# Second-product expert weights in row pairs, and the usual order for the last two experts

## The chip, the cores and the metric

The kernel runs on one core of a Trainium2 chip. The metric is the device time of one launch in microseconds (us); lower is better. The core has five engines with a queue of instructions each: TensorE (PE, its weight loads are PEld), VectorE (DVE), ScalarE (ACT), GpSimd (POOL) and SyncE (SP). SP does no arithmetic here and issues nearly all transfers from memory; 16 DMA engines carry them out.

## What is computed

One layer of a diffusion backbone on 256 tokens (128 of a prompt, 128 of a sample) of width 1024: a mixer (state-space scan and convolution), then a mixture of 32 experts of which each token uses 4, then a final norm. The change touches the experts alone:

```python
def expert_step(acc, e):
    w_gu_e, b_gu_e, w_down_e, b_down_e, w_tok = e
    g, u = jnp.split(t @ w_gu_e + b_gu_e, 2, axis=-1)      # first product, 1024 x 2048
    g = jnp.minimum(g, SWIGLU_LIMIT)
    u = jnp.clip(u, -SWIGLU_LIMIT, SWIGLU_LIMIT)
    act = (u + 1.0) * g * jax.nn.sigmoid(SWIGLU_ALPHA * g)
    out = act @ w_down_e + b_down_e                        # second product, 1024 x 1024
    return acc + w_tok[:, None].astype(out.dtype) * out, None
```

All weights are float32: 12 MB for each expert, 384 MB in all.

## The kernel before

The mixer takes the first 485 us or so, the experts the rest. Of each expert only the tokens routed to it are computed: `gather_slots` picks up to 64 of them for a pair of experts by a matmul with a 0/1 matrix (`xg`). Then, for expert e, `expert_up` makes the first product (line 1238, tiles `e..pgu`, 64 matrix products of 128x64 by 128x512 as the trace counts them, and four for the bias at line 1243), `overflow` tests on every engine whether more tokens are left (a branch, line 1343; the pass behind it runs for expert 11 alone in this trace), and `expert_act` makes `gm` on DVE and ACT (lines 1251 to 1255). `gm` holds 64 tokens by 1024 channels as 128 partitions by 512: the upper 64 partitions are the second half of the channels.

`transposed` (lines 1286 and 1287) turns `gm` round with four PE transposes into the PSUM tile `e..pat`, and ACT copies that to `e..aT`. `down_products` (line 1299) makes the second product into `e..py`, 32 matrix products as the trace counts them. `keep_y` (line 1307) copies `py` into the tile `y` of the pair, one half on ACT and one on DVE. `scatter_pair` (line 1274, tile `pst`, copied to `sT`) and `add_pair` (line 1314, tiles `e..pc`, added into `xT` by DVE at line 1184) put a pair's results back to their tokens. In the usual order the second product of expert e-1 stands on PE ahead of the first product of expert e, and the results of a pair are put back two experts later. From expert 2 on a scheduler sets the order on the engines at build time; `finale` is written out by hand for PE.

The weights come in pieces of 1 MB, twelve to an expert, into 22 slots that are used in turn: pieces 0 to 7 are 128 rows of the first matrix (8 KB on each partition in one run), pieces 8 to 11 are 256 rows of the second. A second-product piece has rows p and p+128 of its 256 on partition p, so two runs of 4 KB. SP issues piece after piece; each issue waits until the piece eight issues back has landed and until the slot is free.

The last two experts are different. The order of the loads is: first product of 30, first product of 31, second product of 30, second product of 31. The second matrix of expert 31 comes by columns: each of its four pieces holds two blocks of 128 columns and all 1024 rows, in 512-byte runs, by four transfers. `finale` makes the first product of 31 ahead of the second product of 30, and then the second product of 31 in four column blocks (`down_rows`, line 1479, tile `lastpy`). After each block `finish` copies it to `y`, puts 256 columns back to their tokens (line 1488, tile `pcl`), adds them into `xT` on DVE, and squares (line 1491, tile `sql`) and scales `xT` (lines 1495 on ACT, 1497 on POOL). So `finish` of one block runs beside the products of the next. Then come the sums of the squares (`pssl`), the norm's factor on POOL (`rf`, line 183), its broadcast (`rbf`), the last multiplications on DVE and five stores.

Of the kernel before, what the change touches and what calls it, by code (L numbers as in the profile page):

```python
# [63 lines left out]
def hybrid_step(ctx, tc, A):  # L64
# [314 lines left out]
    def load_piece(e, c, t=None):  # L379
        if t is None:  # L380
            t = ready.pop((e, c), None)
            if t is not None:
                npc[0] += 1
                return t
            t = next_slot(f"w{e}_{c}")
        if c < 8:
            npc_ins[0] = nc.sync.dma_start(t, w_gu[0, e, c * P:(c + 1) * P, :])
            return t.unsqueeze(1)
        if e == NE - 1:

            t = t.rearrange("p (i k n) -> p i k n", i=2, n=P)
            for k in (0, 4):
                for i in range(2):
                    c0 = (c - 8 + 4 * i) * P
                    nc.sync.dma_start(t[:, i, k:k + 4], w_dn[0, e, k * P:(k + 4) * P, c0:c0 + P].rearrange("(k p) n -> p k n", p=P))
            return t
        t = t.rearrange("p (k n) -> p k n", k=2)
        src = w_dn[0, e, (c - 8) * 256:(c - 7) * 256, :].rearrange("(k p) n -> p k n", p=P)
        nc.sync.dma_start(t, src)
        return t  # L400

    def open_slots(n):
# [12 lines left out]
    early = [0, 1, 2, NSLOT - 3, NSLOT - 2, *range(3, NSLOT - 3)]  # L415

    def load_expert(e):

        if e == NE - 1:
            return last_up + [load_piece(e, c) for c in range(8, 12)]  # L420
        w = [load_piece(e, c) for c in range(8)]
        if e == NE - 2:
            last_up.extend(load_piece(e + 1, c) for c in range(8))
        return w + [load_piece(e, c) for c in range(8, 12)]

    last_up = []
    first_in = []

    def weight_blocks():
# [742 lines left out]
    sm = ctx.enter_context(tc.tile_pool(name="sm", bufs=1))  # L1172

    open_slots(NSLOT - 3 - len(mx))
    def down_cols(e, w, k, c0, wd):

        if e == NE - 1:
            return [w[8 + c // P % 4][:, c // 512, k, :] for c in range(c0, c0 + wd, P)]
        return [w[8 + k // 2][:, k % 2, c0:c0 + wd]]

    def add_gated(k, s, x):

        sl = slice(s * P, (s + 1) * P)
# [96 lines left out]
    def transposed(gm, name, m, tag="aT", bufs=1):  # L1280

        wd = D * m // P
        pat = bank("E", name + "pat", 1)[:, 0:wd]
        aT = sm.tile([P, 512], F32, name=name + "aT", tag=tag, bufs=bufs)[:, 0:wd]
        for c in range(wd // P):
            PE.transpose(pat[:, c * P:(c + 1) * P], gm[:, c * P:(c + 1) * P], ident)  # L1286
        S.copy(aT, pat)  # L1287
        return [aT[:, a:a + m] for a in (k * P % wd + k * P // wd * m for k in range(KC))]

    def down_products(e, at, w, py, m, swap, ks=range(KC)):  # L1290

        nq = P // m
        wd = D // nq
        for k in ks:
            for q in range(nq):
                parts = down_cols(e, w, k, (q ^ swap) * wd, wd)
                n = wd // len(parts)
                for i, part in enumerate(parts):
                    last = PE.matmul(py[m * q:m * q + m, i * n:(i + 1) * n], at[k], part,  # L1299
                                     start=(k == 0 and i == 0), stop=(k == KC - 1), skip_group_check=True)  # L1300
        return last

    def keep_y(ys, py, swap, cols=slice(0, 512)):
# [45 lines left out]
    def overflow_pass(e, w, over, n):  # L1349
        m, nq, wd = OVER, P // OVER, D * OVER // P  # L1350
        V.tensor_scalar(over, over, -float(OVER), None, op0=ALU.add)

        gx = sm.tile([P, 2, m], F32, name=f"gx{n}", tag="g1", bufs=1)
        for s in range(2):
            V.tensor_scalar(gx[:, s], iof[:, 0:m], over[:, s:s + 1], None, op0=ALU.is_equal)
        px = bank("C", f"px{n}", 2)
        for s in range(2):
            for q in range(nq):
                PE.matmul(px[m * q:m * q + m, 0:wd], gx[:, s], h2[:, s, q * wd:(q + 1) * wd],
                          start=(s == 0), stop=(s == 1), skip_group_check=True)  # L1360
        xs = sm.tile([P, wd], F32, name=f"xs{n}", tag="um", bufs=1)
        V.tensor_copy(xs, px[:, 0:wd])
        pxt = bank("C", f"pxt{n}", 2)
        for c in range(wd // P):
            PE.transpose(pxt[:, c * P:(c + 1) * P], xs[:, c * P:(c + 1) * P], ident)
        xo = sm.tile([P, nq, wd // P, m], F32, name=f"xo{n}", tag="xg", bufs=2)
        S.copy(xo, pxt[:, 0:wd].rearrange("p (c q s) -> p q c s", q=nq, s=m))
        go = expert_act(expert_up(e, xo.rearrange("p q c s -> p (q c) s"), w, over_banks(f"{n}pgu", 2), m), n, m, tag="go")
        sg = sm.tile([P, 2, nq, m], F32, name=f"so{n}", tag="um", bufs=1)
        slots_of([sg[:, s] for s in range(2)], e, [over[:, s:s + 1] for s in range(2)])  # L1370
        pst = bank("E", f"pso{n}", 1)
        for s in range(2):
# [5 lines left out]
        down_products(e, transposed(go, n, m), w, py, m, 0)  # L1378
# [15 lines left out]
    def new_y(e):  # L1394
        return [sm.tile([P, 512], F32, name=f"y{e}{q}", tag=f"y{q}", bufs=1) for q in range(2)]

    def down(e):
        if e % 2 == 0:
            ys[e] = new_y(e)
        gm, w = acts.pop(e)  # L1400
        py = bank("D", f"e{e}py", 1)
        last = down_products(e, transposed(gm, f"e{e}", CAP), w, py, CAP, e % 2)
        keep_y(ys[e - e % 2], py, e % 2)
        return last

    def up(e):
# [6 lines left out]
    def expert(e):  # L1413
# [28 lines left out]
        if e % 2 == 0:  # L1442
            if e:
                last = add_pair(e - 2)
            if e == 24:
                add_bias()
        else:
            gather_slots(e + 1)

    w = last = mores = None  # L1450
    for e in range(NE - 1):

        with tc.manual_schedule(engines={mybir.EngineType.PE}) if e < 2 else ExitStack():
            expert(e)


    def finale():
        e = NE - 1
        w = load_expert(e)
        gm, w_1 = acts.pop(e - 1)  # L1460
        banks = expert_up(e, xgs.pop(e), w, up_banks(e, f"e{e}pgu"), CAP, last)
        overflow(e, w, mores[e % REGS])
        at_1 = transposed(gm, f"e{e - 1}", CAP, "xg", 2)
        gm = expert_act(banks, f"e{e}", CAP)
        y = new_y(e - 1)
        py = bank("D", f"e{e - 1}py", 1)
        down_products(e - 1, at_1, w_1, py, CAP, 0, range(4))
        at = transposed(gm, f"e{e}", CAP, "xg", 2)
        down_products(e - 1, at_1, w_1, py, CAP, 0, range(4, KC))
        keep_y(y, py, 0)  # L1470
        pss = bank("E", "pssl", 1)
        py = [bank("BD"[c % 2], f"lastpy{c // 2}", 1) for c in range(2)]
        products = pair_products(scatter_pair(e - 1), y)
        sq = next_slot("sql").rearrange("p (k t) -> p k t", t=T)

        def down_rows(c, ks):
            for k in ks:
                for q in range(2):
                    PE.matmul(py[c % 2][CAP * q:CAP * (q + 1), c * P:(c + 1) * P], at[k], w[8 + c][:, 1 - q, k, :],  # L1479
                              start=(k == 0), stop=(k == KC - 1), skip_group_check=True)  # L1480

        def finish(c):

            cs = slice(c * P, (c + 1) * P)
            keep_y(y, py[c % 2], 1, cs)
            pc = bank("C", f"pcl{c}", 2)
            for i, k in enumerate((c, c + 4)):
                PE.matmul(pc[:, i * T:(i + 1) * T], *products[k], start=True, stop=True)  # L1488
# [23 lines left out]
        down_rows(3, range(KC))  # L1512
        finish(2)
        finish(3)
        for k in (0, 2, 6, 3, 7):
# [97 lines left out]
```

## Time and profile before

| what | us |
|---|---|
| median of 3 runs (lowest, highest) | 1470.7 (1467.85, 1472.33) |
| the profiled execution, its own time | 1469.36 |
| its span, first to last instruction | 1467.6 |
| PE busy in the span | 1352.0 (92%) |
| DVE, ACT, POOL busy | 593.2, 338.1, 108.3 |
| read from memory | 498.26 MB, 343 GB/s over the span |

A busy PE in this table is not PE at its peak, since the ends of pipelined matrix products are modelled. A wait is listed with the engine that waited and what ended it; a name with a q is an engine's queue of instructions, which branches, issues and waits while the engine itself is idle. PEclk is the granted clock of TensorE as a share of 2.4 GHz: 1.00, or 0.50 at its lower level of 1.2 GHz.

### The profile page before, as it was taken

How to read it: one execution, taken by the hardware profiler on the slowest of the kernel's cores; microseconds unless marked ns; L12 is line 12 of the kernel's file. 1: busy time of each engine (PE TensorE's matmuls, PEld its weight loads, DVE VectorE, ACT ScalarE, POOL GpSimd, SP SyncE). 2: the span in 40 equal slices, each digit the busy share in tenths (PEclk: the TensorE clock that was granted, in tenths of full speed). 3: DMA queues.
4: the chain of work that ended last, by engine and by line, in shares of the span. 5: the costliest groups of instructions: out<-in, count | busy, mean ns of one | idle time of the engine just before them, and what ended most of it. 6: DMA issues, size and time to landing. Idle time of an engine off the chain costs nothing. (4 is left out here: it accounts for less than half of the span.)

```text
span 1467.6 us, 21473 instructions
## 1 busy us (share of the span) xinstructions
PE 1352.0 (92%) x8627; PEld 799.2 (54%) x8627; DVE 593.2 (40%) x1265; ACT 338.1 (23%) x636; POOL 108.3 (7%) x121
## 2 busy tenths in 40 slices
PE   6998999999999899999999779999899999989997
PEld 3887989889999443443343334343433343334434
DVE  4864879897776312222132113212312123221323
ACT  2544656565754110000010000000000000000102
POOL 1112314421002100000000000000000000000001
PEclk9999999999999899999999988999999999999998
DMA  9996565646897799999999699999999999999993
GB/s 367 281 275 190 194 239 212 244 167 210 316 327 290 289 407 411 415 412 416 416 413 415 269 372 382 416 416 416 413 414 417 415 415 415 416 415 417 415 365 111
DMA packets 132359, 506.48 MB, mean 345 GB/s; under 512 B 9827, under 2 KB 45283, under 8 KB 94307
## 3 DMA queue, kind: packets, MB, share of 16 engines
q1 hardware_dynamic: 129314, 497.72, 87.4%
q10 hardware_dynamic: 2880, 6.60, 1.3%
q8 instruction: 99, 1.62, 0.5%
q14 instruction: 66, 0.53, 0.1%
HBM read 498.26 MB, written 5.64 MB: 343 GB/s over the span
## 5 line engine op out<-in xcount | busy, mean ns | idle before, releaser
L291 DVE TENSOR_TENSOR wl<-win,wh 128x1024 fp32r<-128x1024 f32 (+1 forms) x84 | 101.2, 1216 | 33.7 <-ACT wh L290 28.3
L290 ACT CAST wh<-win 128x1024 fp32r<-128x1024 f32 (+1 forms) x84 | 83.9, 1009 | 73.0 <-PE pbc L318 19.2
L1501 POOL TENSOR_TENSOR sql<-sql 128x256 f32<-128x256 f32 x3 | 2.2, 727 | 971.1 <-ACT sql L1491 971.1
L711 POOL TENSOR_TENSOR m<-m_half,adt 128x512 fp32r<-128x512 f32 x32 | 43.2, 1368 | 86.6 <-PE pss L714 86.6
L318 PE MATMUL pxs<-hT,wh 128*128 128x256 f32 x256 | 37.5, 291 | 0.0
L318 PE MATMUL pz<-hT,wh 128*128 128x256 f32 x256 | 37.3, 291 | 0.0
L318 PE MATMUL pgt<-hT,wh 128*128 128x256 f32 x256 | 36.0, 287 | 0.6 <-ACT wh L290 0.6
L318 PE MATMUL pbc<-hT,wh 128*128 128x256 f32 x256 | 35.6, 287 | 0.0
L318 PEld LDWEIGHTS pxs<-hT,wh 128*128 128x128 f32 x256 | 32.5, 190 | 3.6 <-issue 2.8
L318 PE MATMUL pso<-yhl,wh 128*128 128x256 f32 x256 | 34.1, 284 | 0.0
L318 PEld LDWEIGHTS pz<-hT,wh 128*128 128x128 f32 x256 | 33.0, 193 | 1.8 <-issue 1.8
L318 PEld LDWEIGHTS pgt<-hT,wh 128*128 128x128 f32 x256 | 32.4, 191 | 2.6 <-issue 1.9
L318 PEld LDWEIGHTS pbc<-hT,wh 128*128 128x128 f32 x256 | 32.2, 190 | 1.9 <-issue 1.7
L318 PEld LDWEIGHTS pso<-yhl,wh 128*128 128x128 f32 x256 | 32.1, 192 | 0.0
L318 PE MATMUL pglu<-hT,wh 128*128 128x256 f32 x192 | 25.9, 285 | 0.0
L215 PE MATMUL pm<-ada,sc__170 128*32 128x512 f32 x80 | 15.4, 830 | 10.1 <-DMA ada<-in_w_ada 10.1
L318 PEld LDWEIGHTS pglu<-hT,wh 128*128 128x128 f32 x192 | 24.0, 192 | 0.7 <-issue 0.5
L291 DVE TENSOR_TENSOR wl<-wso,wh 128x1024 fp32r<-128x1024 f32 x16 | 19.4, 1218 | 7.2 <-ACT wh L290 7.1
L694 ACT ACTIVATE gd<-gm,dtT 128x128 f32<-128x128 f32 x64 | 20.7, 408 | 5.2 <-DVE gm L685 5.2
L695 DVE SCALAR_TENSOR_TENSOR gd<-gm,dtT,gd 128x128 f32<-128x128 f32 x64 | 20.9, 375 | 1.6 <-ACT gd L694 1.2
L290 ACT CAST wh<-wso 128x1024 fp32r<-128x1024 f32 x16 | 16.7, 1046 | 13.7 <-PE pso L318 10.8
L1243 PEld LDWEIGHTS <-sel 96*64 96x64 bf16 (+1 forms) x136 | 8.8, 110 | 19.4 <-issue 19.2
(1026 smaller groups left out, 2666.3 us busy)
## 6 DMA issues: line engine op xcount, KB each, us to landing
w<-in_w_gu SPq DMA_DIRECT2D x256, 1024.0 KB, 19.0
w<-in_w_down SPq DMA_DIRECT2D x124, 1024.0 KB, 16.3
win<-in_w_in_pack SPq DMA_DIRECT2D x38, 1024.0 KB, 5.5
ada<-in_w_ada SPq DMA_DIRECT2D x10, 1024.0 KB, 10.2
wso<-in_w_ssd_out SPq DMA_DIRECT2D x8, 1024.0 KB, 6.4
im<-dru SPq DMA_DIRECT2D x16, 312.0 KB, 8.1
wcf<-in_w_conf_out SPq DMA_DIRECT2D x4, 1024.0 KB, 9.1
wo<-in_w_o SPq DMA_DIRECT2D x4, 1024.0 KB, 9.1
```

What stands on the lines that cost most here:

```text
L215: PE.matmul(out[32 * j:32 * j + 32, :], sc_[:, 4 * r + j, 6 - 2 * c:38 - 2 * c], part[:, j, :], start=(start and r == 0), stop=(stop and r ...
L290: S.copy(hi[:, ks, 0:m], w[:, ks])
L291: V.tensor_tensor(lo[:, ks, 0:m], w[:, ks], hi[:, ks, 0:m], ALU.subtract)
L318: last_wo[0] = PE.matmul(out, w[:, k, 0:n], m[:, k, :], start=first and i == 0, stop=last and i == len(order) - 1, skip_group_check=True)
L694: S.activation(gd[s][:, h, :], gm[:, 0, s, :], AF.Copy, scale=dtT[:, 0, s, c0:c0 + 1])
L695: V.scalar_tensor_tensor(gd[s][:, h, :], gm[:, 1, s, :], dtT[:, 0, s, 32 + c0:33 + c0], gd[s][:, h, :], op0=ALU.mult, op1=ALU.add)
L711: G.tensor_tensor(m4[d], m_half[:, d, None, None, :].to_broadcast([P, 2, 4, 64]), ac[d], ALU.mult)
L1243: PE.matmul(banks[i][m * q:m * q + m, 0:wd], sel3[:, e:e + 1].to_broadcast([96, m]), b3[:, c0:c0 + wd], start=False, stop=True, skip_group ...
L1501: G.tensor_tensor(sq[:, 0], sq[:, 0], sq[:, k], ALU.add)
```

## The change

Every second-product piece now has rows 2p and 2p+1 of its 256 rows on partition p, one run of 8 KB, for all 32 experts. To match, a transpose takes every second channel of `gm`: the even ones of 256 for one block, the odd ones for the next. The loads by columns of expert 31, the changed order of loads, the early first product of 31 and the second product by column blocks are all taken out. Expert 31 goes through the usual loop; `finish` follows on one whole `py`.

```diff
@@ load_piece
-        if e == NE - 1:
-
-            t = t.rearrange("p (i k n) -> p i k n", i=2, n=P)
-            for k in (0, 4):
-                for i in range(2):
-                    c0 = (c - 8 + 4 * i) * P
-                    nc.sync.dma_start(t[:, i, k:k + 4], w_dn[0, e, k * P:(k + 4) * P, c0:c0 + P].rearrange("(k p) n -> p k n", p=P))
-            return t
         t = t.rearrange("p (k n) -> p k n", k=2)
-        src = w_dn[0, e, (c - 8) * 256:(c - 7) * 256, :].rearrange("(k p) n -> p k n", p=P)
-        nc.sync.dma_start(t, src)
+        nc.sync.dma_start(t, w_dn[0, e, (c - 8) * 256:(c - 7) * 256, :].rearrange("(p k) n -> p k n", k=2))
@@ load_expert
-        if e == NE - 1:
-            return last_up + [load_piece(e, c) for c in range(8, 12)]
-        w = [load_piece(e, c) for c in range(8)]
-        if e == NE - 2:
-            last_up.extend(load_piece(e + 1, c) for c in range(8))
-        return w + [load_piece(e, c) for c in range(8, 12)]
+        return [load_piece(e, c) for c in range(12)]
@@ transposed
-            PE.transpose(pat[:, c * P:(c + 1) * P], gm[:, c * P:(c + 1) * P], ident)
+            c0 = c // 2 * 256
+            PE.transpose(pat[:, c * P:(c + 1) * P], gm[:, c0 + c % 2:c0 + 256:2], ident)
@@ down
+        if e < NE - 1:
+            keep_y(ys[e - e % 2], py, e % 2)
+        else:
+            last_y.append(py)
@@ the loop over experts
-    for e in range(NE - 1):
+    for e in range(NE):
@@ finale
-        banks = expert_up(e, xgs.pop(e), w, up_banks(e, f"e{e}pgu"), CAP, last)
-        overflow(e, w, mores[e % REGS])
-        at_1 = transposed(gm, f"e{e - 1}", CAP, "xg", 2)
-        gm = expert_act(banks, f"e{e}", CAP)
...
+        down(NE - 1)
+        y, py = ys[NE - 2], last_y[0]
...
-            keep_y(y, py[c % 2], 1, cs)
+            keep_y(y, py, 1, cs)
...
-        down_rows(0, range(KC))
-        down_rows(1, range(4))
         finish(0)
         add_squares(4)
-        down_rows(1, range(4, KC))
-        down_rows(2, range(4))
         finish(1)
         add_squares(1, 5)
-        down_rows(2, range(4, KC))
-        down_rows(3, range(KC))
         finish(2)
         finish(3)
```

Line numbers in the changed kernel are 21 to 42 lower; on every engine the order up to the end of expert 30's first product is the one of before. The first place is PE behind that first product, before the change (`e28pc` puts the pair 28 and 29 back; `e31pgu` is the first product of 31):

```order
L1314 MATMUL e28pc_16367<-sT_15766,y_15728 128x256 x2
L1314 MATMUL e28pc_16374<-sT_15766,y_15729 128x256 x2
L1314 MATMUL e28pc_16381<-sT_15766,y_15729 128x256 x2
L1238 MATMUL e31pgu_16410<-w_0_16059,xg_16020 64x512 x2
L1238 MATMUL e31pgu_16411<-w_0_16059,xg_16020 64x512 x2
```

The same place on PE after it:

```order
L1292 MATMUL e28pc_16352<-sT_15766,y_15728 128x256 x2
L1266 MATMUL e30pat<-ident,e30gm 128x128 x4
L1292 MATMUL e28pc_16359<-sT_15766,y_15729 128x256 x2
L1277 MATMUL e30py<-w_8_16059,e30aT 64x512 x4
L1277 MATMUL e30py<-w_9_16061,e30aT 64x512 x4
L1277 MATMUL e30py<-w_10_16063,e30aT 64x512 x4
L1277 MATMUL e30py<-w_11_16065,e30aT 64x512
L1292 MATMUL e28pc_16366<-sT_15766,y_15729 128x256 x2
L1277 MATMUL e30py<-w_11_16065,e30aT 64x512 x3
L1253 MATMUL pst_16429<-ident,sg_16424 128x128 x4
L1217 MATMUL e31pgu_16436<-w_11_16065,xg_16020 64x512 x2
```

The transposes and the second product of 30 moved from behind the first product of 31 to ahead of it. The second place is DVE in `finish`, before (the copies to `y` are one each for a column block, the additions into `xT` four each):

```order
L1307 COPY y_16696<-lastpy_16725 64x128
L1184 SCALAR_TENSOR_TENSOR xT<-pcl_16766,fin,xT 128x128 x4
L1307 COPY y_16696<-lastpy_16726 64x128
L1184 SCALAR_TENSOR_TENSOR xT<-pcl_16796,fin,xT 128x128 x4
L1307 COPY y_16696<-lastpy_16725 64x128
L1307 COPY y_16696<-lastpy_16726 64x128
L1184 SCALAR_TENSOR_TENSOR xT<-pcl_16835,fin,xT 128x128 x4
L1184 SCALAR_TENSOR_TENSOR xT<-pcl_16848,fin,xT 128x128 x4
```

and after:

```order
L1285 COPY y_16396<-e31py 64x128 x3
L1163 SCALAR_TENSOR_TENSOR xT<-pcl_16713,fin,xT 128x128 x4
L1285 COPY y_16396<-e31py 64x128
L1163 SCALAR_TENSOR_TENSOR xT<-pcl_16727,fin,xT 128x128 x4
L1163 SCALAR_TENSOR_TENSOR xT<-pcl_16742,fin,xT 128x128 x4
L1163 SCALAR_TENSOR_TENSOR xT<-pcl_16755,fin,xT 128x128 x4
```

Three of the four copies moved ahead of the first additions, and no product stands between the blocks any more. On ACT, which makes the other half of each copy, all four copies now stand ahead of the first square, and each waits for DVE's copy of the block before it.

## Rows read from the trace of the kernel before

**Rows 1.** The page: memory traffic in 40 equal slices of the span

```profile
GB/s 367 281 275 190 194 239 212 244 167 210 316 327 290 289 407 411 415 412 416 416 413 415 269 372 382 416 416 416 413 414 417 415 415 415 416 415 417 415 365 111
```

**Rows 2.** Stretches: us, busy time of five engines, granted clock, DMA share, GB/s

```profile
1015.00:1017.50 2.50, 2.50 (x16) 0.79 (x14) 0.00 (x0) 0.00 (x0) 0.00 (x0) 1.00 1.02 423
...
1032.50:1035.00 2.50, 2.11 (x19) 1.87 (x18) 0.62 (x1) 0.79 (x2) 0.00 (x0) 1.00 1.03 413
...
1387.00:1390.50 3.50, 3.50 (x18) 3.50 (x19) 1.18 (x3) 0.00 (x0) 0.00 (x0) 0.54 1.00 417
...
1434.00:1436.00 2.00, 1.70 (x12) 0.65 (x8) 0.53 (x1) 0.00 (x0) 0.00 (x0) 1.00 1.01 276
```

**Rows 3.** SP's issues: start, us, line, tile, count

```profile
1000.58 9.40 SPq L387 DMA_DIRECT2D w<-in_w_gu  x8
1012.14 17.22 SPq L399 DMA_DIRECT2D w<-in_w_down  x4
...
1359.70 38.95 SPq L387 DMA_DIRECT2D w<-in_w_gu  x16
```

**Rows 4.** Transfers: KB each, median us from issue to landing

```profile
w<-in_w_gu SPq DMA_DIRECT2D x256, 1024.0 KB, 19.0
```

**Rows 5.** What PE waited for, 900 to 1400 us: total, times, longest

```profile
PE xg26p L1215 <- DVE g L1325: 2.0, 1, 2.0
...
PE e21py L1299 <- ACT e21aT L1287: 0.7, 1, 0.7
```

**Rows 6.** PE in order of time, experts 28 and 29: start, us, [idle before]

```profile
1356.04 0.60 PE L1243 MATMUL e28pgu<-b,sel 96*64 96x512 bf16 x4
...
1359.65 0.63 PE L1286 MATMUL e28pat<-ident,e28gm 128*128 128x128 f32 x4 [0.32 <-DVE e28gm L1255]
...
1370.53 13.95 PE L1238 MATMUL e29pgu<-w,xg 128*64 128x512 f32 x64
...
1393.53 7.09 PE L1299 MATMUL e29py<-w,e29aT 128*64 128x512 f32 x32 [0.73 <-ACT e29aT L1287]
```

**Rows 7.** PE in order of time, experts 30 and 31

```profile
1400.45 13.90 PE L1238 MATMUL e30pgu<-w,xg 128*64 128x512 f32 x64
1414.18 0.60 PE L1243 MATMUL e30pgu<-b,sel 96*64 96x512 bf16 x4
...
1420.89 13.95 PE L1238 MATMUL e31pgu<-w,xg 128*64 128x512 f32 x64
1434.67 0.60 PE L1243 MATMUL e31pgu<-b,sel 96*64 96x512 bf16 x4
```

**Rows 8.** The chain that ended last: start, us, what

```profile
1452.14 2.77 PE lastpy L1479 x48
1454.91 1.07 PE pcl L1488 x4
```

**Rows 9.** PE in order of time: work behind a pause

```profile
1087.72 3.81 PE L1215 MATMUL xg20p<-g,h 128*128 128x128 f32 x32 [2.01 <-DVE g L1325]
...
1386.93 5.44 PE L1215 MATMUL xg30p<-g,h 128*128 128x128 f32 x32 [2.01 <-DVE g L1325]
```

**Rows 10.** PE behind the branch of expert 26

```profile
1297.17 3.75 PE L1314 MATMUL e24pc<-sT,y 128*128 128x256 f32 x8 [5.58 <-DVEq L1343]
1300.72 1.06 PE L1286 MATMUL e26pat<-ident,e26gm 128*128 128x128 f32 x4
```

**Rows 11.** All engines in order of time, the end of the kernel

```profile
1454.95 0.26 ACT L1307 COPY y<-lastpy 64x128 f32<-64x128 f32 x1 [0.23 <-PE lastpy L1479]
1455.25 0.29 DVE L1307 COPY y<-lastpy 64x128 f32<-64x128 f32 x1 [1.45 <-ACT y L1307]
1456.01 2.16 DVE L1184 SCALAR_TENSOR_TENSOR xT<-pcl,fin,xT 128x128 f32<-128x128 f32 x8 [0.47 <-PE pcl L1488]
...
1456.65 1.97 ACT L1491 ACTIVATE sql<-xT 128x256 f32<-128x256 f32 x4 [1.44 <-DVE xT L1184]
...
1459.72 0.72 POOL L183 TENSOR_TENSOR rf<-rfv,mhalf 128x2 f32<-128x2 f32 x1 [0.73 <-DVE rfv L181]
```

More of the change, by code (lines that the diff above doesn't have):

```diff
@@ L417, in load_expert @@
     def load_expert(e):
-        if e == NE - 1:
-            return last_up + [load_piece(e, c) for c in range(8, 12)]
-        w = [load_piece(e, c) for c in range(8)]
-        if e == NE - 2:
-            last_up.extend(load_piece(e + 1, c) for c in range(8))
-        return w + [load_piece(e, c) for c in range(8, 12)]
-    last_up = []
+        return [load_piece(e, c) for c in range(12)]
     first_in = []
@@ L1174, in hybrid_step @@
     open_slots(NSLOT - 3 - len(mx))
[L1175 to L1179, printed above, removed]
     def add_gated(k, s, x):
@@ L1285, in transposed, with down_products @@
         for c in range(wd // P):
-            PE.transpose(pat[:, c * P:(c + 1) * P], gm[:, c * P:(c + 1) * P], ident)
+            c0 = c // 2 * 256
+            PE.transpose(pat[:, c * P:(c + 1) * P], gm[:, c0 + c % 2:c0 + 256:2], ident)
         S.copy(aT, pat)
         return [aT[:, a:a + m] for a in (k * P % wd + k * P // wd * m for k in range(KC))]
-    def down_products(e, at, w, py, m, swap, ks=range(KC)):
+    def down_products(at, w, py, m, swap):
         nq = P // m
         wd = D // nq
-        for k in ks:
+        for k in range(KC):
             for q in range(nq):
[L1296 to L1300, printed above, removed]
+                c0 = (q ^ swap) * wd
+                last = PE.matmul(py[m * q:m * q + m, 0:wd], at[k], w[8 + k // 2][:, k % 2, c0:c0 + wd],
+                                 start=(k == 0), stop=(k == KC - 1), skip_group_check=True)
         return last
@@ L1377, in overflow_pass @@
         py = bank("D", f"{n}py", 1)
-        down_products(e, transposed(go, n, m), w, py, m, 0)
+        down_products(transposed(go, n, m), w, py, m, 0)
         S.copy(yo, py[:, 0:wd])
@@ L1401, in down @@
         py = bank("D", f"e{e}py", 1)
-        last = down_products(e, transposed(gm, f"e{e}", CAP), w, py, CAP, e % 2)
-        keep_y(ys[e - e % 2], py, e % 2)
+        last = down_products(transposed(gm, f"e{e}", CAP), w, py, CAP, e % 2)
+        if e < NE - 1:
+            keep_y(ys[e - e % 2], py, e % 2)
+        else:
+            last_y.append(py)
         return last
@@ L1446, in expert @@
                 add_bias()
-        else:
+        elif e < NE - 1:
             gather_slots(e + 1)
     w = last = mores = None
-    for e in range(NE - 1):
+    last_y = []
+    for e in range(NE):
         with tc.manual_schedule(engines={mybir.EngineType.PE}) if e < 2 else ExitStack():
@@ L1457, in finale @@
     def finale():
-        e = NE - 1
-        w = load_expert(e)
-        gm, w_1 = acts.pop(e - 1)
-        banks = expert_up(e, xgs.pop(e), w, up_banks(e, f"e{e}pgu"), CAP, last)
-        overflow(e, w, mores[e % REGS])
-        at_1 = transposed(gm, f"e{e - 1}", CAP, "xg", 2)
-        gm = expert_act(banks, f"e{e}", CAP)
[L1465 to L1470, printed above, removed]
+        down(NE - 1)
+        y, py = ys[NE - 2], last_y[0]
         pss = bank("E", "pssl", 1)
-        py = [bank("BD"[c % 2], f"lastpy{c // 2}", 1) for c in range(2)]
-        products = pair_products(scatter_pair(e - 1), y)
+        products = pair_products(sT[NE - 2], y)
         sq = next_slot("sql").rearrange("p (k t) -> p k t", t=T)
[L1476 to L1480, printed above, removed]
         def finish(c):
             cs = slice(c * P, (c + 1) * P)
-            keep_y(y, py[c % 2], 1, cs)
+            keep_y(y, py, 1, cs)
             pc = bank("C", f"pcl{c}", 2)
```

## The prediction

> **What bounds the kernel now.** I read the memory traffic first, because the change is about transfers. From the fifteenth slice on it stands at 407 to 417 GB/s in all but a few [rows 1], and in short stretches the share of the DMA engines is 1.02 or 1.03 [rows 2]: they are never free. That looks like the bound. The second view says it is not. Between 900 and 1400 us, where PE makes some sixteen experts, the list of PE's waits holds no transfer: it waits 2.0 us for DVE at the gather of a pair and 0.7 for ACT's copy [rows 5], and 5.58 once at a branch [rows 10]. The third view shows why. The first product of expert 30 begins at 1400.45 [rows 7]; its eight pieces are the first eight of the sixteen issues that began at 1359.70 and took 38.95 us [rows 3], so they were issued by about 1379 and, at a median of 19.0 us to landing [rows 4], all lay there by about 1398. The first of them had landed about 22 us before PE touched it. PE needs 13.95 us for eight pieces [rows 7] and the transfers about 20 (8 x 2.5 us, 1 MB at 416 GB/s), so a lead of about 6 us would be enough.
>
> So the DMA engines are full and still ahead: PE reads slots that were filled long ago. What sets the time is the order on PE, with short pauses for the other engines, up to the last product, and after it the chain over copies, additions, squares and the norm. At the end it is the same: the chain that ended last runs over PE to 1455.98 [rows 8].
>
> **The change part by part: the body.** Up to the end of expert 30's first product no instruction on PE, DVE, ACT or POOL changes its place. What is new there: 124 pieces move as 8 KB runs and not as two of 4 KB. The price of that is seen where both kinds of run move alone. First-product pieces issued at 1000.58 to 1009.98 and second-product pieces issued from 1012.14 on [rows 3] land some 19 us later; the stretch at 1015.0 (8 KB runs) moved 423 GB/s, the one at 1032.5 (4 KB runs) 413 [rows 2]. That is 2.48 against 2.54 us for 1 MB, about 0.06 us a piece and 7 us in all, and all of it is hidden: it makes a lead longer that is already long enough. I take 0.
>
> The four transposes of each expert now read every second channel, with a step of 8 bytes. They are on PE's path: 0.63 us for four [rows 6]. No row here reads an operand of PE with such a step. From below it costs nothing, since the number of columns is the same; from above I take the slowest four transposes of this kind in the trace, 1.06 us at the lower clock [rows 10], so 0.43 more for each of 32 experts, 14 us. A gain is excluded: the same four instructions read the same elements. I take 0 since each element is still read once and the weight load of a transpose lies mostly beside the one before. The Trainium skill, page "SBUF — State Buffer", section "Door 1: The DMA port swizzle", says that accesses which hit a 16-byte line at least twice run at full bandwidth; two float32 channels 8 bytes apart share such a line, so by that page the cost is 0, and no run here shows it yet.
>
> **The end, PE.** Now the order around experts 30 and 31. Before, from the end of 30's bias products (1414.18 + 0.60 = 1414.78) to the start of 31's first product (1420.89) it took 6.11 us [rows 7]. After, the order there is the one of experts 28 and 29: from 1356.64 to 1370.53 it took 13.89 us [rows 6]. So the first product of 31 starts at 1428.67 and, with 14.38 us to the end of its bias products as before [rows 7], ends at 1443.05. Its weights: before, the last of them was issued by 1398.65 [rows 3] and landed by about 1418 [rows 4]. The order of loads now puts them 4 pieces later, about 10 us, so they land by about 1428 and the last is needed at 1440.7. The four second-product pieces follow, the last near 1439; the first is needed at 1447.4, the last after 1452. On SP the moved loads pass only each other. The cover is over 10 us; without it each us of lateness would count.
>
> Then a cost that was hidden. Before, the activation of 31 ran beside the second product of 30; now PE has nothing else. From the end of the bias products to the transposes it took 3.01 us at expert 28 (1356.64 to 1359.65), of which other PE work filled most; then 0.63 for the transposes, 0.73 for ACT's copy, and 7.09 for the second product [rows 6]. The last product ends at 1443.05 + 11.46 = 1454.51; before it was 1452.14 + 2.77 = 1454.91 [rows 8]. The sum on PE is -0.40 us: the early order of before bought almost nothing, because its column blocks were no faster than whole products and the `finish` products of two blocks stood between them.
>
> **The clock.** PE pauses for 3.0 us and again for 0.73. After pauses of 2.0 us the same 32 gather products took 3.81 us at one pair and 5.44 at another [rows 9]; in the second the granted clock was 0.54 on the mean, so mostly 1.2 GHz [rows 2]. After 5.58 us the eight products behind it took 3.75 us [rows 10], and four transposes 0.43 more than usual. So this pause may cost 0 to 2.3 us; I take 1.6 (5.44 less 3.81), since 3.0 us lie beyond 2.0, where it already happened.
>
> **The end, `finish`.** From the last product's end (call it D) to the norm's factor on POOL it took 1459.72 - 1454.91 = 4.81 us, because two of four blocks were done. Now all four begin at D. The copies go in turn, 0.26 on ACT, then 0.29 on DVE, 0.62 for a block with the gaps [rows 11], since each engine's copy waits for the other's: DVE's third ends at D+1.9, while `pcl` of block 0 (1.06, [rows 8]) ends at D+1.7. DVE then adds: four additions take 1.1 us (2.16 for eight, [rows 11]). Block 0 to D+3.0, the fourth copy to 3.3, block 1 to 4.4, block 2 to 5.5; block 3's products need the bank of block 1, so they run from 4.45 to 5.5, and the last additions end at D+6.65. Before, additions ended at 1456.01 + 2.16, D+3.3. ACT has eight squares and four scalings in turn, about 0.42 us each (0.49 for a square in the row, with waits); it starts at D+2.5 and is held by the additions, so the last square is done at D+7.5, before at D+3.7. From the last square to `rf` it took 1.1 us (1458.62 to 1459.72); so `rf` starts at D+8.6. POOL's three additions and two scalings fit ahead of that. The term is 8.6 - 4.8 = +3.8 us. All behind `rf` stays.
>
> **The sum.** -0.4 + 1.6 + 3.8 = +5.0 us: a span of 1472.6, its run 1474.4 (1.76 us lie outside the span). The profiled run is 1.3 us under the median of the runs; the sum is put on the median: 1475.7.
>
> **The rivals.**
> *The transfers set the time after all.* For it: the DMA share of 1.02. Then 124 pieces save 7 us in the body, and expert 31's second matrix, 4.2 MB in 512-byte runs at 276 GB/s in a stretch with a share of 1.01 [rows 2], comes at 416: 15.2 us become 10.1. `finish` still costs its 3.8; the new order and the pause don't count, as PE waits anyway. -7 - 5.1 + 3.8 is -8.3: 1462.4. Against it: no transfer among PE's waits, and a lead of 22 us where 6 do. It decides from the point where PE finds a slot empty. The Trainium skill, page "DMA: Bandwidth & Descriptors", section "Anatomy of one DMA", fits the time of a transfer issued by GpSimd by its bytes alone, 2 us and bytes at 436 GB/s; by it the run length would save nothing, even in this rival; the stretches above, 413 against 423, disagree. Chance 7%.
> *The stepped transposes cost.* 14 us more on PE's path from above, so up to 1490; half of it 1482. Chance 6%.
> *The clock stays up and ACT and DVE keep closer than I count.* +3.4 or less: 1473 to 1474, inside 0.3%. Chance 30%.
> *The lower clock also meets `finish`.* The four `pcl` of 1.06 would take up to twice that, and three of them lie on the chain: 3 us more, 1478.7. Chance 8%.
> *A branch stalls at the end.* At expert 26 DVE stayed in the branch for some 5 us and PE waited 5.58 [rows 10], without any data to wait for. The code behind expert 30 is other code now, and such a stall at 31 would cost about 5 more: 1480.7. Chance 4%.
> *The row pairs don't become 8 KB runs.* Then the body's 0 stays 0; nothing changes in the sum.
>
> **How the numbers follow.** The forecast, +4 to +6.5 us, has 45%. The bound of what a measurement of this kernel can tell from no change is 0.3%, 4.4 us: 1466.3 to 1475.1. The forecast's upper part, the cold `finish`, the transposes and the stall lie beyond it: 55% for slower. The third rival and the forecast's lower part make 38% within. Faster, 7%, is the first rival. The range from 1471 to 1481 leaves out the transfers, most of the transposes' case and the scatter of a median.
>
> **What would show it.** In the changed trace: PE's waits in the expert stage without a transfer, and pairs of experts as long as before; SP waiting more for PE and less for landings; transposes of 0.63; the first product of 31 at about 1428.7; a pause of 3.0 us behind it, and the granted clock there; `rf` 8.6 us behind the last product. Transposes above 0.7 or PE waiting for a weight piece would prove me wrong.

## The result, and the profile after

| what | before | after |
|---|---|---|
| median of 12 runs each on one chip (us) | 1467.88 | 1477.77 |
| the same again, 23 and 12 runs (us) | 1468.45 | 1477.55 |
| profiled execution, its own time / its span | 1469.36 / 1467.6 | 1479.28 / 1477.5 |

The ratio is 1.0057 (95% interval 1.004 to 1.0073), and 1.0054 (1.0038 to 1.0071) the second time: the changed kernel is slower by about 0.55%, 8 to 10 us. The forecast was 1475.7 in a range from 1471 to 1481. So the side and the range were right, but +5.0 us was forecast and some 9 came. That the median lies in the range is in part luck: the forecast set out from 1470.7, while the kernel before ran at 1467.88 beside the changed one, and 3 of the 9 us come from a place that the forecast did not touch (below).

The page of the changed kernel first: PEclk in 40 slices, memory traffic, and packets by size. The line by itself is that of the kernel before.

```profile
PEclk9999999999999899999999989999999999999998
...
GB/s 367 278 276 190 198 239 202 239 186 194 334 330 279 291 418 417 418 408 419 418 418 419 191 398 383 416 419 419 418 418 420 417 418 420 418 419 417 419 335 30
DMA packets 108613, 506.46 MB, mean 343 GB/s; under 512 B 9634, under 2 KB 36898, under 8 KB 54178
```

```profile
DMA packets 132359, 506.48 MB, mean 345 GB/s; under 512 B 9827, under 2 KB 45283, under 8 KB 94307
```

The row pairs did to the transfers what they should: from the 26th slice to the 38th the plateau went from 413 to 417 GB/s [rows 1] to 416 to 420, and the kernel takes longer all the same. The last slice moves 30 GB/s where it moved 111: the slices are longer, the last weights come earlier, and nothing waits for them.

Now PE in order of time, from the end of expert 30's first product to the end (start, us, engine, line, tile, shape, count, idle before and what ended it). It answers to [rows 7] and [rows 8].

```profile
1417.77 0.60 PE L1222 MATMUL e30pgu<-b,sel 96*64 96x512 bf16 x4
1419.09 1.97 PE L1292 MATMUL e28pc<-sT,y 128*128 128x256 f32 x8 [0.72 <-DVEq L1321]
1421.38 0.72 PE L1266 MATMUL e30pat<-ident,e30gm 128*128 128x128 f32 x4 [0.32 <-DVE e30gm L1234]
1422.41 1.10 PE L1292 MATMUL e28pc<-sT,y 128*128 128x256 f32 x4 [0.32 <-DVE xT L1163]
1423.44 6.22 PE L1277 MATMUL e30py<-w,e30aT 128*64 128x512 f32 x26
1429.60 1.13 PE L1292 MATMUL e28pc<-sT,y 128*128 128x256 f32 x4
1430.66 1.93 PE L1277 MATMUL e30py<-w,e30aT 128*64 128x512 f32 x6
1432.52 0.66 PE L1253 MATMUL pst<-ident,sg 128*128 128x128 f32 x4
1433.11 13.95 PE L1217 MATMUL e31pgu<-w,xg 128*64 128x512 f32 x64
1446.89 0.60 PE L1222 MATMUL e31pgu<-b,sel 96*64 96x512 bf16 x4
1450.42 0.72 PE L1266 MATMUL e31pat<-ident,e31gm 128*128 128x128 f32 x4 [2.92 <-DVE e31gm L1234]
1451.81 8.78 PE L1277 MATMUL e31py<-w,e31aT 128*64 128x512 f32 x32 [0.68 <-ACT e31aT L1267]
1461.28 1.99 PE L1452 MATMUL pcl<-sT,y 128*128 128x256 f32 x8 [0.69 <-DVE y L1285]
1463.77 1.10 PE L1452 MATMUL pcl<-sT,y 128*128 128x256 f32 x4 [0.49 <-DVE xT L1163]
1465.23 1.10 PE L1452 MATMUL pcl<-sT,y 128*128 128x256 f32 x4 [0.36 <-DVE xT L1163]
1467.05 2.39 PE L196 MATMUL pssl<-one,sql 128*128 128x1 f32 x20 [0.71 <-POOL sql L1465]
1470.50 0.69 PE L191 MATMUL rbf<-ident,rf 128*128 128x128 f32 x2 [1.06 <-POOL rf L183]
```

No weight piece is waited for. Before, PE's longest pause between 31's bias products and the last product was the 0.73 us for ACT's copy; now it pauses 2.92 us, the product behind it takes 8.78 instead of 7.09, and from the last product's end (D = 1451.81 + 8.78 = 1460.59) to the broadcast of `rf` it is 9.91 us. Before, the last product ended at 1454.91 [rows 8] and `rbf` began at 1460.50, 5.59 later:

```profile
1456.67 2.77 PE L196 MATMUL pssl<-one,sql 128*128 128x1 f32 x20
1460.50 0.69 PE L191 MATMUL rbf<-ident,rf 128*128 128x128 f32 x2 [1.06 <-POOL rf L183]
```

All traces of this study cut at the same marks give a table that the experiments below share. The columns: start of expert 0's first product; from there to expert 12's; from there to the end of 30's bias products; and the tail behind that: to 31's first product, that product, to D, from D to `rbf`, from `rbf` to the end, and their sum (us).

| kernel | start | 0 to 12 | 12 to 30 | to 31 | 31 | to D | to rbf | to end | tail |
|---|---|---|---|---|---|---|---|---|---|
| before | 488.5 | 372.6 | 553.65 | 6.11 | 14.39 | 19.63 | 5.59 | 7.08 | 52.8 |
| after | 488.9 | 375.9 | 553.54 | 14.74 | 14.39 | 13.10 | 9.91 | 6.99 | 59.1 |
| after, second trace | 489.2 | 375.7 | 553.52 | 14.73 | 14.39 | 13.10 | 9.91 | 6.99 | 59.1 |
| row pairs only | 494.8 | 370.2 | 553.34 | 6.11 | 14.39 | 19.72 | 5.42 | 6.81 | 52.5 |
| order only | 494.2 | 372.8 | 553.67 | 14.73 | 14.39 | 13.01 | 9.91 | 6.97 | 59.0 |
| pause filled | 489.5 | 373.2 | 553.55 | 14.73 | 14.39 | 11.76 | 9.91 | 6.73 | 57.5 |
| blocks | 495.1 | 372.9 | 553.54 | 14.73 | 14.39 | 15.61 | 5.42 | 6.58 | 56.7 |
| pause filled and blocks | 487.7 | 373.2 | 550.34 | 14.73 | 14.39 | 14.30 | 5.42 | 6.83 | 55.7 |
| early slots | 493.4 | 368.9 | 539.02 | 6.19 | 14.39 | 22.61 | 5.42 | 6.81 | 55.4 |
| early slots, row pairs | 487.9 | 367.9 | 535.39 | 6.20 | 14.39 | 23.32 | 5.43 | 7.05 | 56.4 |
| early slots, whole change | 489.2 | 368.7 | 535.57 | 15.03 | 14.85 | 14.42 | 10.03 | 7.12 | 61.5 |
| the same with blocks | 488.2 | 368.5 | 535.74 | 15.04 | 14.85 | 16.72 | 5.42 | 6.56 | 58.6 |

Two things stand out ahead of any experiment. Between expert 12 and expert 30 the change moved nothing: 553.65 and 553.54. And the +9.9 us of span are +6.3 in the tail, +0.4 at the start and +3.3 in experts 0 to 11.

### The profile page after: what moved, and what is told of

Same layout as the page of the kernel before. It is cut to its first block, busy times and chain, and to the rows that moved or that the text cites. A ratio compares the mean times of both kernels' runs of the same rounds, so it can differ in the third digit from the quotient of the medians.

```text
span 1477.5 us, 21271 instructions
## 1 busy us (share of the span) xinstructions
PE 1358.7 (92%) x8531; PEld 801.3 (54%) x8531; DVE 593.4 (40%) x1265; ACT 337.6 (23%) x636; POOL 108.3 (7%) x121
## 2 busy tenths in 40 slices
DMA packets 108613, 506.46 MB, mean 343 GB/s; under 512 B 9634, under 2 KB 36898, under 8 KB 54178
```

## The experiments

### Which part costs: the row pairs alone, the order alone, the change again

The row pairs without the new end (the lines that hand `e` to `transposed` are left out here). Its counterpart, `order only` in the table, is the changed kernel with the old rows in a piece and plain transposes:

```diff
-        src = w_dn[0, e, (c - 8) * 256:(c - 7) * 256, :].rearrange("(k p) n -> p k n", p=P)
+        src = w_dn[0, e, (c - 8) * 256:(c - 7) * 256, :].rearrange("(p k) n -> p k n", k=2)
@@ transposed
...
-            PE.transpose(pat[:, c * P:(c + 1) * P], gm[:, c * P:(c + 1) * P], ident)
+            c0 = c // 2 * 256
+            src = gm[:, c0 + c % 2:c0 + 256:2] if e < NE - 1 else gm[:, c * P:(c + 1) * P]
+            PE.transpose(pat[:, c * P:(c + 1) * P], src, ident)
```

> The kernel before with one part of the change: the second-product pieces of experts 0 to 30 come in row pairs (8 KB runs) and their transposes take every second channel; expert 31, its loads by columns, the order of loads and the end stay as before. My theory: the 7 us saved on transfers are hidden and the stepped transposes cost nothing that counts, so the time is that of before, ratio 0.998 to 1.002, with four transposes at 0.63 to 0.65 us and the rest of the differences only in which gather products meet the lower clock (1.6 us each). Rival A: the 3.6 us by which the changed kernel is later at expert 30 belong to the layout: ratio 1.0025 or more. Rival B: transfers set the time: about -7 us, ratio 0.995.

Measured: 1471.02 us beside 1471.54 for before, ratio 1.0003 (0.9986 to 1.0019). My theory held, and both rivals fell, since the interval leaves out 1.0025 and 0.995. Its transfers ran at about 419 GB/s on the plateau, and the time did not follow.

> The changed kernel with the old rows in a second-product piece (p and p+128, 4 KB runs) and plain transposes: only the last two experts are changed against before. My theory: the end alone costs what the traces show there, +6.3 us (2.1 up to the last product, 4.2 in the copies, additions and squares behind it), ratio 1.0043 (1.003 to 1.0055), so 1.4 or so of each thousandth less than the changed kernel. Rival: the 3.6 us in the body come with the new order or with code that lies at other addresses, not with the layout: +9.9 us, ratio 1.0067, as in the changed kernel.

Measured: 1480.66, ratio 1.0057 (1.0037 to 1.0076). The interval holds the 1.0043 of my theory and the 1.0067 of the rival, so the times alone don't decide. Its trace speaks for the theory: the tail is 59.0 (+6.2), expert 12 to 30 is 553.67, experts 0 to 11 took 372.8, and what is left, 5.7 us, had been lost ahead of the first expert (494.2), in a part that neither kernel changes. Four traces start late, at 493.4 to 495.1, and the others at 487.7 to 489.5, whatever the layout and the end; the kernel with row pairs alone is one of the four, and the median of its runs was that of before. So I take a late start for a draw that any kernel may get, though no kernel has a trace of both kinds here. The whole tail belongs to the order and the pieces of the last two experts.

The unchanged changed kernel, run once more:

> The changed kernel itself, beside new runs of the kernel before and with a second trace. In the first trace 6.3 us of the difference lie behind expert 30's bias products and 3.6 ahead of them. My theory: the 6.3 are the change and come again within 0.3 us (->product of 31 14.7, to the last product 13.1, to the broadcast of rf 9.9), as does the stretch from expert 12 to expert 30, 553.3 to 553.7 us with and without the change; what lies ahead (the start of the experts, 488 to 495 us, and experts 0 to 11, 370 to 376) is another draw of the same scatter as in the kernel before. Ratio 1.0043 to 1.006. Rival: the part ahead of expert 12 is systematically longer in the changed kernel: again 376 us for experts 0 to 11.

Measured: ratio 1.0054 (1.0038 to 1.0071). Tail and experts 12 to 30 came again to 0.02 us. Experts 0 to 11 took 375.7 again, so the rival has a point as well. In both traces of the changed kernel the gathers of pairs 8 and 10 took 5.43 to 5.44 us; in the six other traces without early slots they took 3.81, and four of these have the changed kernel's end, four its layout, three both. So neither part of the change explains it, nor both together. What decides stays open.

### What the tail is made of: the pause and `finish`

Three idle products in the pause ahead of expert 31's transposes:

```diff
     def finale():
+        fill = bank("C", "fill", 2)
+        w_31 = acts[NE - 1][1]
+        for i in range(3):
+            PE.matmul(fill, ident, w_31[0][:, 0, 0:512], start=True, stop=True)
         down(NE - 1)
```

> The changed kernel with three products more on PE (identity by 128x512 columns of a piece that lies there) in the pause of 2.9 us ahead of the transposes of expert 31; their result is used by nothing. My theory: 31's second product takes 8.78 us and not 7.09 because PE paused, so with the pause filled it takes 7.1 and the time falls by 1.7 us, ratio to before about 1.0012 below that of the changed kernel measured beside the same runs of before, if the three products end ahead of the transposes. Rival: the second product of 31 is slower for another reason (its place, its operands): it stays at 8.8 and the time is the changed kernel's or some tenths more.

Measured: 1476.17, ratio 1.0042 (1.0028 to 1.0057), 0.0012 to 0.0015 below the changed kernel's two ratios; the intervals overlap, and the trace decides. PE in order of time:

```profile
1444.73 0.60 PE L1222 MATMUL e31pgu<-b,sel 96*64 96x512 bf16 x4
1446.05 2.81 PE L1443 MATMUL fill<-w,ident 128*128 128x512 f32 x6 [0.72 <-DVEq L1321]
1448.70 0.63 PE L1266 MATMUL e31pat<-ident,e31gm 128*128 128x128 f32 x4
1450.00 7.09 PE L1277 MATMUL e31py<-w,e31aT 128*64 128x512 f32 x32 [0.68 <-ACT e31aT L1267]
```

Two stretches that cover the second product of 31, of the changed kernel and then with the pause filled (length, five engines' busy time, granted clock, DMA share, GB/s):

```profile
1451.80:1460.60 8.80, 8.78 (x32) 2.61 (x32) 0.00 (x0) 0.00 (x0) 0.00 (x0) 0.81 0.00 0
```

```profile
1450.00:1457.10 7.10, 7.09 (x32) 2.21 (x32) 0.00 (x0) 0.00 (x0) 0.00 (x0) 1.00 0.00 0
```

The same 32 products take 8.78 us at a mean granted clock of 0.81 (so partly at 1.2 GHz) behind a pause of 2.92, and 7.09 at 1.00 when PE was busy ahead of them. The rival that they are slow in themselves falls. From D to `rbf` both traces show 9.91: `finish` is not held by PE's clock.

The second product of 31 in column blocks again, out of whole-row pieces, with `finish` of a block between them:

```diff
...
-            keep_y(y, py, 1, cs)
+            keep_y(y, py[c % 2], 1, cs)
...
+        def down_rows(c, ks):
+            for k in ks:
+                for q in range(2):
+                    c0 = (1 - q) * 512 + c * P
+                    PE.matmul(py[c % 2][CAP * q:CAP * (q + 1), c * P:(c + 1) * P], at[k], w[8 + k // 2][:, k % 2, c0:c0 + P],
+                              start=(k == 0), stop=(k == KC - 1), skip_group_check=True)
+        down_rows(0, range(KC))
+        down_rows(1, range(4))
         finish(0)
...
```

> The changed kernel, but the second product of expert 31 is made in four column blocks from the row-pair pieces, with finish of a block between the next blocks' products as in the kernel before. It undoes the finish part of the change alone. My theory: the factor rf comes 4.8 us behind the last product again and not 9.1, but the last product ends some 3 us later (four blocks of 1.97 and two pairs of finish products of 1.1 between them against 7.09 for the whole), so 1.3 us in all are won: +5 against before, ratio 1.0034. Rival: the blocks hide the whole finish at no price: -4.3 us, +2 against before, ratio 1.0014. Rival: the blocks run at the lower clock too and are slower than the whole product by more than 4.3: no gain, ratio 1.0043 or more.

Measured: 1473.88, ratio 1.0032 (1.0015 to 1.0049). The stretch from D to `rbf` is 5.42 again, 4.5 less; D is 2.5 later. 2.0 us are won net up to `rbf`. My theory had 1.3, and the direction of both terms was right; the trace speaks against both rivals, as the blocks have a price and still win. And both remedies at once:

> The changed kernel with both remedies: the pause ahead of expert 31's transposes is filled with three products, and the second product of 31 is made in column blocks with finish between them. My theory: the two terms are separate, the clock (1.3 to 1.6 us up to the last product) and finish (4.5 less 2.5 for the blocks, part of which was the lower clock), so they add: the stretch behind expert 30's bias products is 6.3 - 1.6 - 2.4 = 2.3 us longer than before and at most 3; ratio to before 1.001 to 1.003. Rival: the blocks run at the lower clock even behind a filled pause: 3.9 us or more longer.

Measured: 1471.67, ratio 1.0018 (0.9999 to 1.0038); the tail is 55.7, +2.9 against before. PE in order of time, first with blocks alone, then with the pause filled as well:

```profile
1453.53 0.71 PE L1266 MATMUL e31pat<-ident,e31gm 128*128 128x128 f32 x4 [2.92 <-DVE e31gm L1234]
1454.92 4.51 PE L1473 MATMUL lastpy<-w,e31aT 128*64 128x128 f32 x48 [0.68 <-ACT e31aT L1267]
1459.36 1.13 PE L1454 MATMUL pcl<-sT,y 128*128 128x256 f32 x4
```

```profile
1443.75 0.63 PE L1266 MATMUL e31pat<-ident,e31gm 128*128 128x128 f32 x4
1445.06 2.84 PE L1476 MATMUL lastpy<-w,e31aT 128*64 128x128 f32 x48 [0.68 <-ACT e31aT L1267]
1447.83 1.13 PE L1457 MATMUL pcl<-sT,y 128*128 128x256 f32 x4
```

The lower clock costs the same in either form of the product, 4.51 - 2.84 = 1.67 and 8.78 - 7.09 = 1.69. The terms are separate and they add. Up to `rbf` the filled pause won 1.3 us (1.69 on the product and 0.09 on the transposes, less 0.44 by which the three products outlast the pause), the blocks 2.0, and both 3.3. Against before 2.9 remain in the tail: 3.3 more ahead of D and 0.4 less behind it. The 550.34 us from expert 12 to 30 in this trace are 3.2 fewer than in the others because two stretches met the higher clock, the work behind the branch of expert 12 and the gather of pair 14; neither remedy stands there.

### Where row pairs do pay: PE made faster

The body's answer, "hidden", holds only while PE is slower than the transfers. To try the other side, the 0/1 matrix of a gather is made one pair ahead on DVE, which takes PE's pause of 2.0 us ahead of it away:

```diff
...
+        g1 = slots_in(e + 1) if e % 2 and 2 < e < NE - 1 else None
         if e >= 2:
             banks = up(e)
...
-            gather_slots(e + 1)
+            gather_slots(e + 1, g1 or slots_in(e + 1))
```

> The kernel before with the 0/1 matrix of a gather made one pair ahead on DVE (its tile is shared with the overflow pass before, which takes another tile now); nothing else is changed. It takes the pause of 2.0 us ahead of 13 or 14 gathers away. My theory: with no pause ahead of them no gather meets the lower clock either (5.44 against 3.81 us), so each pair is 2.0 to 3.6 us shorter, 26 to 34 us in all, until the lead of the transfers is used up: the first piece of expert 30 lay there 19.6 us before its use, and about 6 are needed, so behind the overflow of expert 11 no more than some 14 us can be won, and some 12 ahead of it: -26 us, ratio 0.982, and PE waits for weight pieces in the last experts. Rival: the lower clock at the gathers has nothing to do with the pause ahead of them: some of the gathers still take 5.44 us, -12 to -20 us. Rival: transfers set the time already: 0.

Measured: 1455.16, ratio 0.9885 (0.9862 to 0.9908), some 16 us and not 26. Ahead of expert 12 only pairs 8, 10 and 12 had such a pause, and 3.8 us were won there, not 12. Behind it 14.6 us were won, as the lead allowed, and the tail lost 2.6. The list of PE's waits between 900 and 1400 us shows what took the pauses' place: the weight pieces, and DVE at the even experts, whose activation now stands behind the branch.

```profile
PE e28pgu L1238 <- DMA w<-in_w_gu: 3.5, 5, 1.2
PE e26pgu L1238 <- DMA w<-in_w_gu: 2.1, 2, 1.5
PE e30pgu L1238 <- DMA w<-in_w_gu: 1.7, 3, 0.6
...
PE e26pat L1286 <- DVE e26gm L1255: 1.5, 1, 1.5
```

Now the row pairs on top of it:

> The run before this one (the 0/1 matrix of a gather made a pair ahead) with the row pairs for experts 0 to 30 as well. My theory: here PE has used up the lead of the transfers in the last experts, so the 2.48 instead of 2.54 us for a second-product piece is worth something: 2 to 6 us less than without the row pairs, ratio to before 0.978 to 0.981. Rival: the row pairs are worth nothing even where PE waits for pieces (the transfers' time goes by bytes alone): the same time as without them. Rival: PE never comes to wait for a piece: the same time as without them, and no transfer among PE's waits.

Measured: 1450.83, ratio to before 0.9865 (0.9839 to 0.9891), the fastest kernel of the study. The 0.978 to 0.981 that I expected stood on the 26 us of the run before and missed with them. The two intervals overlap, but the traces are plain: from expert 12 to 30 it took 539.0 without row pairs and 535.4, 535.6 and 535.7 in the three kernels with them. From [rows 2], 18 x 4 pieces at 0.06 us were to be worth 4.3; 3.3 to 3.6 were measured, against one trace without row pairs. In that one trace the gather of pair 24 also stops for 1.50 us in its middle, and 1.9 of the 3.6 us first show there. The transfers' own rate says that the gain does not hang on this stop. Here is the same stretch without and with row pairs (length, five engines' busy time, granted clock, DMA share, GB/s):

```profile
920.00:1360.00 440.00, 408.20 (x1994) 165.61 (x1992) 106.33 (x282) 35.03 (x60) 0.00 (x0) 1.00 1.02 415
```

```profile
920.00:1360.00 440.00, 411.17 (x2008) 167.90 (x2004) 106.24 (x281) 35.00 (x60) 0.00 (x0) 1.00 1.01 418
```

The DMA engines were full in both, PE waited for weight pieces from expert 24 on in both, and 418 for 415 GB/s is 3.2 us in these 440. One gather of the run with row pairs stands for the clock as well, against the pause of 2.0 us and the 5.44 us that the same gather took before:

```profile
1328.78 5.44 PE L1215 MATMUL xg28p<-g,h 128*128 128x128 f32 x32 [2.01 <-DVE g L1325]
```

```profile
1298.90 0.60 PE L1243 MATMUL e27pgu<-b,sel 96*64 96x512 bf16 x4
1299.90 3.81 PE L1215 MATMUL xg28p<-g,h 128*128 128x128 f32 x32 [0.39 <-PEq L1348]
```

Then the whole change on this faster kernel, without and with blocks:

> The whole change on the kernel with the 0/1 matrix of a gather made a pair ahead, where PE waits for weight pieces in the last experts. My theory: here the shorter transfers count: the row pairs are worth 4.3 us as measured, and expert 31's second matrix comes in 10 us and not in 15, so its last piece lands some 5 us earlier than with the row pairs alone; D is then set by PE at about 1432 on the scale of the run with early slots and row pairs, and rf follows 9.1 behind: some 0.5 to 2.2 us over that run, and 2 to 4 us under the run with early slots alone. So the same change makes this kernel faster and the tuned one slower. Ratio to before 0.986 to 0.989. Rival: the end costs 6.3 us here too: 6 us over the run with early slots and row pairs, ratio 0.991.

> The run before this one with the second product of expert 31 in column blocks as well. My theory: the same 1.3 us less as without the early slots: about level with the run with early slots and row pairs alone, ratio to before 0.985 to 0.988. Rival: no gain, as the blocks cost what finish wins.

Measured: 1456.85, ratio 0.9908 (0.9892 to 0.9925), and with blocks 1455.04, 0.9906 (0.9884 to 0.9928). My theory fell; the rival held. The end costs 5.1 us of tail here too (61.5 against 56.4). I had counted on expert 31's second matrix to be late by columns, but with early slots and row pairs PE waits for it only 2.6 us in all, while the pause ahead of the transposes grows to 3.61 and the product to 9.04 us. With blocks the tail falls by 2.9, to 58.6, more than the 1.3 us of my theory, but it is not level with early slots and row pairs alone (56.4); the medians, six runs each, don't resolve the gain, and the ratio lies outside the 0.985 to 0.988 that I expected.

## Why the prediction was right, and where its size was off

**What bounds the kernel: right.** The transfers became faster and the time did not; the rival in which they set the time needed an empty slot, and there was none. With PE made faster it came true: 3.3 to 3.6 us for the row pairs where 4.3 were worked out. One of the signs that I had named came the other way round: from 900 to 1360 us SP waited 203 us for landings before and 234 after, and for PE 152 and 129. Why was not tried.

**The body, 0: right in its mechanism.** The row pairs alone gave 1.0003. The records of the transposes became longer: expert 27's four took 0.60 us before and 0.64 after, 28's and 30's 0.72 where 28's took 0.63 [rows 6]. That is above the 0.7 that I had named as a sign against me, though far from the upper bound of 1.06. On PE's path it is not seen. Expert 27 before, and then after:

```profile
1334.06 0.60 PE L1286 MATMUL e27pat<-ident,e27gm 128*128 128x128 f32 x4
1335.38 7.09 PE L1299 MATMUL e27py<-w,e27aT 128*64 128x512 f32 x32 [0.73 <-ACT e27aT L1287]
```

```profile
1337.65 0.64 PE L1266 MATMUL e27pat<-ident,e27gm 128*128 128x128 f32 x4
1338.97 7.09 PE L1277 MATMUL e27py<-w,e27aT 128*64 128x512 f32 x32 [0.69 <-ACT e27aT L1267]
```

From the transposes' start to the second product's it is 1.32 us in both, and experts 12 to 30 are 553.34 with row pairs alone and 553.65 without. The Trainium skill, page "SBUF — State Buffer", section "Door 1: The DMA port swizzle", has accesses that hit a 16-byte line at least twice at full bandwidth; the trace agrees with that on the path, while the records of the four transposes are 0.04 to 0.09 us longer.

**The end on PE: the step that failed is "the order there is the one of experts 28 and 29".** From 30's bias products to 31's first product 13.89 was forecast and 14.74 measured, and it is 14.73 in all traces with that order. The pattern was taken from expert 28, whose second product is cut by `e26pc` at another place (after, PE in order of time):

```profile
1365.30 5.37 PE L1277 MATMUL e28py<-w,e28aT 128*64 128x512 f32 x24
1370.60 1.13 PE L1292 MATMUL e26pc<-sT,y 128*128 128x256 f32 x4
1371.66 1.94 PE L1277 MATMUL e28py<-w,e28aT 128*64 128x512 f32 x8
```

That is 5.37 + 1.94 = 7.31, and for expert 30, cut after 26 and not after 24, 6.22 + 1.93 = 8.15: here is the missing 0.85, to 0.01. The starts of the single records show why. As a rule they come in twos, a few ns apart, and a two follows the one before it after 0.43 us. The program issues the two halves of the columns in turn, two records each, and the cut after 26 stands between two halves (13 of 16 issued). Four records then start alone, at 1428.64, 1429.08, 1431.57 and 1432.00, which is four steps of 0.43 where two would do. The rows of the changed order that stand ahead of the prediction already show it: one product from `w_11`, then `e28pc`, then three.

**The clock: right, and it was the largest guess.** 1.6 us were taken between bounds of 0 and 2.3; 1.69 were measured on the product, which took 7.09 again once the pause was filled.

**`finish`: the step that failed is the 1.1 us from the last square to `rf`, taken over from before with "POOL's three additions and two scalings fit ahead of that".** `rf` was to start at D + 8.6; it started at D + 9.13, so the term is 4.3 and not 3.8. The rows of the end of after, all engines:

```profile
1462.50 1.12 DVE L1163 SCALAR_TENSOR_TENSOR xT<-pcl,fin,xT 128x128 f32<-128x128 f32 x4
...
1463.96 2.16 DVE L1163 SCALAR_TENSOR_TENSOR xT<-pcl,fin,xT 128x128 f32<-128x128 f32 x8
...
1466.27 0.73 POOL L1465 TENSOR_TENSOR sql<-sql 128x256 f32<-128x256 f32 x1 [0.26 <-ACT sql L1455]
...
1466.37 1.13 DVE L1163 SCALAR_TENSOR_TENSOR xT<-pcl,fin,xT 128x128 f32<-128x128 f32 x4 [0.25 <-PE pcl L1452]
1466.74 1.21 ACT L1455 ACTIVATE sql<-xT 128x256 f32<-128x256 f32 x3
...
1469.48 0.16 DVE L181 TENSOR_SCALAR rfv<-pssl 128x2 f32<-128x2 f32 x1 [1.98 <-PE pssl L196]
1469.72 0.72 POOL L183 TENSOR_TENSOR rf<-rfv,mhalf 128x2 f32<-128x2 f32 x1 [0.92 <-DVE rfv L181]
```

The additions began at D + 1.91 (1.9 forecast), the third block's ended at D + 5.53 (5.5), the last at D + 6.9 (6.65), the last square at 1466.74 + 1.21, D + 7.36 (7.5). Up to there the sum held. But the sums of squares on PE begin with the tile that POOL adds into, and POOL's third addition ended at 1467.00; the 20 products, 2.39 us, run from 1467.05 to 1469.44, and the last square has been ready since 1467.95. Before, they could begin at 1456.67, 1.95 ahead of the last square (1458.62 [rows 11]). So 1.77 us lie between the last square and `rf` instead of 1.1.

**The sum.** Forecast -0.4 + 1.6 + 3.8 = +5.0. In the tail: +2.1 up to D (0.85 for the split, 1.69 for the clock, the rest as forecast) and +4.3 behind it, +6.3 in all, twice. What lies between 6.3 and the 9.1 to 9.9 of the medians was not in the forecast, and no experiment ties it to a part of the change: in the two traces it is the gathers of pairs 8 and 10, 5.44 us each instead of 3.81, 3.3 us together.

**The rivals.** The lower clock at `finish` did not come (9.91 with the pause filled, too), nor a branch that stalls at the end. That the row pairs don't become 8 KB runs is refuted: 54178 packets under 8 KB and not 94307.

## What to carry to other kernels

A full DMA engine says nothing as long as each slot is filled long before its use: compare landing with use, and expect a cheaper transfer to pay only from the point where the two meet. The last step of a kernel has nothing behind it that hides its waits, so an order that looks like a detour (the next product pulled ahead, the last product in blocks) may be all that covers an activation, a norm or a pause that lowers the clock. When a forecast takes a pattern from a neighbouring step, read the new order row by row to see that the pattern is cut in the same places.

## What the runs showed that was not expected

- Behind the pause of 2.0 us the gathers of pairs 14 to 30 took either 3.81 or 5.40 to 5.44 us, never a value between. In seven of the eight traces without early slots five of the nine were slow (in the eighth four), not always the same: 14, 16, 24, 28, 30 before; 14, 20, 24, 28, 30 with row pairs alone. With the pause gone, those of pairs 14 to 28 took 3.81 to 3.87 in three traces; in the fourth 16 took 3.98 and 24 took 5.57, of which 1.50 are a stop in its middle. So such a pause costs 2.0 us or 3.6. It is not a plain draw: 28 and 30 were slow in all eight traces, 18 and 26 in none. What decides stays open.
- A second product took 7.09 us whole, 7.30 and 7.31 where other work cuts it after 16 or 24 of its 32 recorded products, and 8.15 after 26 or 10 (2.79 + 5.36, early slots with the whole change). In both of the dear cuts four records start alone, in the cheap ones none; a cut moved by one product was not tried.
- The stall of 5.4 to 5.6 us at the branch of expert 26 [rows 10] came at the same place in all eight traces without early slots, whatever the layout and the end, and in none of the four with them. There the first step of the activation stands behind the branch on DVE instead of ahead of it; whether that is the cause was not tried.
